# Matmul with bias and tanh on one core: B's first eight k-tiles as whole 128-partition loads, two of them in float32 over SyncE

## The chip, the cores and the metric

The kernel runs on one core of a Trainium2 chip. The metric is the device time of one execution in microseconds (us); several executions are taken and the median is quoted. The profile shows one execution by engine: PE is the matrix engine (PEld are its weight loads), DVE is VectorE, ACT is ScalarE, POOL is GpSimd, SP is SyncE. POOL and SP do no arithmetic that matters here; they issue DMA. "Span" is the profiled execution from first to last instruction.

## The reference

```python
m, k, n = 4096, 4096, 4096
a = np.random.randn(m, k).astype(np.float32)
b = np.random.randn(k, n).astype(np.float32)
bias = np.random.randn(n).astype(np.float32)

def reference(a, b, bias):
    return np.tanh(np.matmul(a, b) + bias)
```

## The kernel before

PE multiplies in float16. A k-tile is 128 values of k, one on each partition, and there are 32 of them. A is cast to float16 by the load, on GpSimd's queue (the input is float32, and a load of 128 x 1024 of its values counts 256 KB in the profile, two bytes a value), lies in memory as rows, and VectorE transposes it in blocks of 32 x 32 (kernels built on this, e1 for one, give right results). So the rows of A are loaded in four quarters of k, `q`, each into 32 partitions, and B has to follow the same order of k: partition `q*32 + p` of k-tile `t` holds `k = q*1024 + t*32 + p`. A k-tile of B therefore takes four DMAs, each into 32 partitions.

The output is made in four chunks of 1024 columns. In the first chunk nothing is on chip yet. There the first eight row-tiles (128 rows each) are taken in two groups of four, so that PE can work on the k-tiles that have arrived: group 0 runs k-tiles 0 to 7 (64 matmuls) and its sums are put aside, group 1 does the same, then group 0 runs k-tiles 8 to 31, then group 1. After that the main loop takes one row-tile at a time.

```python
    def load_b(bt, n0, t0, nt, q):
        src = b[ds(q * KQ + t0 * QP, nt * QP), ds(n0, NCW)]       # KQ = 1024, QP = 32
        nc.gpsimd.dma_start(
            out=bt[t0 // TB][ds(q * QP, QP), ds(t0 % TB, nt), :],
            in_=src.rearrange("(t p) n -> p t n", p=QP),
        )

    def transpose_a(at, an, mb0, t0, nt):
        nc.vector.transpose(
            at[:, ds(t0, nt), :].rearrange("P t (mb p) -> P mb t p", p=QP),
            an[:, ds(mb0, Q), :].rearrange("P mb (t k) -> P mb t k", k=QP),
        )
    ...
    for i in range(WARM):                                         # 24 matmuls of zeros
        nc.tensor.matmul(warm, zeros[:, :P], zeros, start=i == 0, stop=i == WARM - 1)
    want_a("g0a", 2, 0, 2 * Q, 0, KS)                             # A, row-tiles 0 and 1
    want(lambda: load_b_all(0, 2))                                # B, k-tiles 0 and 1
    want_a("g0b", 2, 2 * P, 2 * Q, 0, KS)                         # A, row-tiles 2 and 3
    for t in range(2, KS, 2):
        want(lambda t=t: load_b_all(t, 2))
    bias_bc = biasp.tile([P, NCW], fp32, name="bias_bc")
    want(lambda: load_bias(bias_bc, 0))
    want_a("g1a", 2, 4 * P, 2 * Q, 0, KS)
    ...
    turn(ats[0], "g0a", 0, 0, KS)                                 # turn: transpose
    turn(ats[1], "g0a", Q, 0, KS)
    across(ps, (0, 1), 0, 2, 0)                                   # row-tiles 0, 1; k-tiles 0, 1
    turn(ats[2], "g0b", 0, 0, KS)
    turn(ats[3], "g0b", Q, 0, KS)
    across(ps, (2, 3), 0, 2, 0)
    across(ps, range(G), 2, KS - 4, 0)
    def aside0(ps, m, j):
        put_aside(ps, m, j)                                       # VectorE: sum + bias
        if (m, j) == (1, 1):
            turn1(0)
    down(ps, KS - 2, KS, aside0)
    turn1(1)
    ...
    def end0(ps, m, j):
        end(ps, m, j)
        if (m, j) == (1, 1):
            turn2(0)
    down(ps, KT - TB, KT, end0)
```

`want` puts a load into GpSimd's queue in this order. The loads of A share three buffers.

## Time and profile before

The median was 1791.72 us (1790.18 to 1792.72, three executions).

| what | before |
|---|---|
| span of the profiled execution | 1789.8 us |
| PE busy | 1779.1 us |
| main loop: 7712 matmuls, busy (mean of a start-to-start 215 ns) | 1657.8 us |
| first real matmul | 11.35 us |
| start of the main loop's 7680 matmuls in the chain of waits | 127.84 us |
| from the end of that stretch to the end of the span | 7.76 us |

The last line is the span less 127.84 + 1654.20 us; the last matmuls of the last tile, which is made in two halves, are in it.

PE is busy to 99%, and 8192 matmuls at 215 ns are 1761 us. All that a change can win without touching the matmuls is in the start and the tail. This is PE's timeline of the start (start in us, length, engine, line, operation, count; in brackets PE's idle time before it and what ended it):

```profile
11.35 3.05 PE L121 MATMUL ps<-b,at 128*128 128x512 f16 x8 [2.90 <-DMA b<-in_b_dram]
15.36 14.06 PE L121 MATMUL ps<-b,at 128*128 128x512 f16 x56 [0.95 <-DVE at L83]
30.12 14.05 PE L121 MATMUL ps<-b,atx 128*128 128x512 f16 x64 [0.71 <-DVE atx L83]
44.01 41.60 PE L121 MATMUL ps<-b,at 128*128 128x512 f16 x192
86.23 4.06 PE L121 MATMUL ps<-b,atx 128*128 128x512 f16 x18 [0.62 <-DVE atx L83]
```

The reader is to see four stretches: group 0's first 64 matmuls from 11.35 to 29.4 us, group 1's from 30.12 us, group 0's second part from 44.01 us and group 1's from 86.23 us. The idle time is before the first matmul, between its halves, and before each of group 1's parts. VectorE's groups of instructions, by shape (busy us, mean ns of one, idle before):

```profile
L83 DVE STREAM_TRANSPOSE at<-an 128x1024 f16<-128x1024 f16 x16 | 18.9, 1220 | 26.7 <-DMA an<-in_a_dram 26.7
```

A transpose of eight k-tiles of one row-tile takes 1.22 us. The windows show what each engine does in the first 10 us; the first line names the columns (busy us and count of each engine); the DMA share exceeds 1 in places, and only the GB/s are used here:

```profile
core 0: us, PE busy (x) PEld busy (x) DVE busy (x) ACT busy (x) POOL busy (x), PEclk, DMA share, GB/s
0.00:5.00 5.00, 3.81 (x9) 1.35 (x10) 0.27 (x1) 1.28 (x1) 3.90 (x11) 1.00 0.53 62
5.00:10.00 5.00, 3.45 (x16) 1.40 (x14) 2.17 (x2) 0.00 (x0) 3.63 (x7) 1.00 1.08 143
13.00:14.00 1.00, 1.00 (x4) 0.22 (x2) 0.00 (x0) 0.00 (x0) 0.85 (x2) 0.50 1.22 216
```

The first 10 us move 62 and 143 GB/s. From 30 us on the same view shows 202 to 208 GB/s in every 10 us up to 80 us. At 13 to 14 us PE's granted clock is 0.50, half of full speed. Finally two DMA issues in POOL's timeline:

```profile
60.72 0.54 POOL L66 DMA_DIRECT2D b<-in_b_dram  x1 [0.69 <-DMA b<-in_b_dram]
...
71.07 0.54 POOL L75 DMA_DIRECT2D an<-in_a_dram  x1 [0.69 <-DMA b<-in_b_dram]
```

The first is the last load of B's tiles 24 to 27. The second is eight places later in the queue, and it waited for a load of B. The chain of waits shows the same step elsewhere: the load issued at 42.83 us landed at 52.91 us and released, 0.28 us later, the issue at 53.19 us, which is eight places behind it. So tiles 24 to 27 had landed at about 70.8 us.

### The profile page before, as it was taken

What the parts mean: (1) busy time and instruction counts of PE and PEld (TensorE: products, weight loads), DVE (VectorE), ACT (ScalarE), POOL (GpSimd) and SP (SyncE); (2) the same over time, 40 slices, a digit from 0 to 9 for tenths busy, and PEclk for the clock granted to TensorE, in tenths of its full rate; (3) what the DMA queues carried; (4) which work ended last, traced back from release to release, by engine and by line L of the source; (5) the groups of instructions that cost most, each with busy time, mean ns of one, the idle gap of its engine ahead of it and who ended that gap; (6) DMA issues with size and microseconds to landing.
All of it is one profiled execution on the core that took longest, in us unless ns stands there. A gap on an engine that the chain in (4) does not pass through costs nothing.

```text
span 1789.8 us, 19352 instructions
## 1 busy us (share of the span) xinstructions
PE 1779.1 (99%) x8248; PEld 807.4 (45%) x8248; DVE 745.0 (42%) x420; ACT 162.7 (9%) x260; POOL 358.0 (20%) x668
## 2 busy tenths in 40 slices
PE   8999999999999999999999999999999999999999
PEld 3444444444444444444444444444444444444444
DVE  5463344334433444334433443344334433444341
ACT  0110000000000000000000000000000000000001
POOL 6422222211222211111132222111111111111100
PEclk9999999999999999999999999999999999999999
DMA  9999887665777865655588777555665555655621
GB/s 182 214 189 189 155 159 147 125 132 114 159 147 144 170 140 108 121 119 124 106 168 156 158 142 142 121 112 107 127 120 112 112 113 109 125 112 111 120 70 41
DMA packets 138630, 238.26 MB, mean 133 GB/s; under 512 B 14769, under 2 KB 27569, under 8 KB 138545
## 3 DMA queue, kind: packets, MB, share of 16 engines
q0 software_dynamic: 101248, 169.91, 56.6%
q1 hardware_dynamic: 37296, 67.13, 10.3%
q8 instruction: 64, 1.05, 0.2%
q14 instruction: 22, 0.17, 0.0%
HBM read 337.64 MB, written 67.11 MB: 226 GB/s over the span
## 4 chain that ended last, share of the span: by engine, by line
PE 95%; DMA 4%; POOL 1%; issue 1%; DVE 0%; ACT 0%; ACTq 0%; DVEq 0%; POOLq 0%
PE ps L321 92%; PE ps L121 2%; DMA b<-in_b_dram 2%; DMA an<-in_a_dram 1%; POOL b L66 0%; DMA bias_bc<-in_bias_dram 0%; POOL an L75 0%; DVE atx L83 0%; ACT o_sb L135 0%; DVE o_sb L132 0%; ACTq L354 0%; DVEq L132 0%; POOLq L343 0%
## 5 line engine op out<-in xcount | busy, mean ns | idle before, releaser
L321 PE MATMUL ps<-b,at 128*128 128x512 f16 x7712 | 1657.8, 378 | 0.0
L321 PEld LDWEIGHTS <-at 128*128 128x128 f16 x7712 | 754.6, 98 | 903.3
L132 DVE TENSOR_TENSOR o_sb<-ps,bias_bc 128x512 f32<-128x512 f32 (+1 forms) x243 | 166.4, 686 | 977.8 <-PE ps L321 764.1
L83 DVE STREAM_TRANSPOSE at<-an 128x4096 f16<-128x4096 f16 (+1 forms) x136 | 551.0, 4056 | 26.7 <-DMA an<-in_a_dram 26.7
L75 POOL DMA_DIRECT2D an<-in_a_dram x524 | 282.8, 547 | 1296.6 <-DVE at L83 1224.4
L135 ACT ACTIVATE o_sb<-o_sb 128x512 f32<-128x512 f32 (+1 forms) x243 | 151.5, 624 | 1505.7 <-DVE o_sb L132 1505.7
L66 POOL DMA_DIRECT2D b<-in_b_dram x136 | 73.2, 542 | 55.2 <-PE ps L321 28.6
L121 PE MATMUL ps<-b,at 128*128 128x512 f16 x256 | 58.6, 391 | 3.9 <-DMA b<-in_b_dram 2.9
L121 PE MATMUL ps<-b,atx 128*128 128x512 f16 x256 | 55.7, 379 | 1.3 <-DVE atx L83 1.3
L121 PEld LDWEIGHTS <-at 128*128 128x128 f16 x256 | 25.3, 100 | 37.1 <-issue 5.7
L121 PEld LDWEIGHTS <-atx 128*128 128x128 f16 x256 | 24.8, 98 | 32.2 <-DVE atx L83 2.7
L132 DVE TENSOR_TENSOR spill<-ps,spill 128x512 f32<-128x512 f32 x16 | 10.7, 684 | 25.7 <-PE ps L121 25.4
L135 ACT ACTIVATE spill<-spill 128x512 f32<-128x512 f32 x16 | 10.0, 630 | 117.2 <-DVE spill L132 117.2
L83 DVE STREAM_TRANSPOSE atx<-an 128x1024 f16<-128x1024 f16 (+1 forms) x8 | 18.3, 2295 | 0.0
L155 DVE TENSOR_TENSOR spill<-ps,bias_bc 128x512 f32<-128x512 f32 x16 | 10.1, 670 | 10.0 <-PE ps L121 10.0
L196 PE MATMUL ps<-zeros 128*128 128x512 f16 x24 | 7.3, 476 | 1.2 <-DVE zeros L193 1.2
L196 PEld LDWEIGHTS <-zeros 128*128 128x128 f16 x24 | 2.8, 118 | 5.2 <-issue 2.5
L90 POOL DMA_DIRECT2D bias_bc<-in_bias_dram x4 | 2.3, 563 | 0.1
L135 ACT ACT_TABLE_LOAD x1 | 1.3, 1283 | 0.7 <-PEq L343 0.7
L193 DVE MEMSET zeros<- 128x256 uint32 x1 | 0.3, 272 | 0.9 <-PEq L343 0.9
L343 POOL MEMSET const-float32-0.0<- 128x1 f32 x1 | 0.1, 98 | 0.2 <-issue 0.2
L343 POOL MEMSET const-bfloat16-1.0<- 128x1 bf16 x1 | 0.1, 101 | 0.0
(2 smaller groups left out, 0.2 us busy)
## 6 DMA issues: line engine op xcount, KB each, us to landing
an<-in_a_dram POOLq DMA_DIRECT2D x492, 256.0 KB, 5.4
out_dram<-o_sb SPq DMA_DIRECT2D x239, 256.0 KB, 4.3
b<-in_b_dram POOLq DMA_DIRECT2D x120, 256.0 KB, 8.9
out_dram<-spill SPq DMA_DIRECT2D x16, 256.0 KB, 6.4
an<-in_a_dram POOLq DMA_DIRECT2D x16, 192.0 KB, 7.8
an<-in_a_dram POOLq DMA_DIRECT2D x16, 128.0 KB, 5.7
b<-in_b_dram POOLq DMA_DIRECT2D x16, 128.0 KB, 5.0
bias_bc<-in_bias_dram POOLq DMA_DIRECT2D x4, 512.0 KB, 8.2
```

What stands on the lines that cost most here:

```text
L66: nc.gpsimd.dma_start(out=bt[t0 // TB][ds(q * QP, QP), ds(t0 % TB, nt), :], in_=src.rearrange("(t p) n -> p t n", p=QP),)
L75: nc.gpsimd.dma_start(out=an[ds(q * QP, QP), :, :], in_=src.rearrange("(mb p) k -> p mb k", p=QP),)
L83: nc.vector.transpose(at[:, ds(t0, nt), :].rearrange("P t (mb p) -> P mb t p", p=QP), an[:, ds(mb0, Q), :].rearrange("P mb (t k) -> P mb t ...
L90: nc.gpsimd.dma_start(out=bias_bc, in_=bass.AP(tensor=src.tensor, offset=src.offset, ap=[[0, P], *src.ap]),)
L121: nc.tensor.matmul(ps, at[:, t, :], bt[t // TB][:, t % TB, ts(j, NB)], start=start, stop=stop)
L132: nc.vector.tensor_tensor(out=o_sb[:, piece], in0=ps[:, piece], in1=addend[:, piece], op=mybir.AluOpType.add)
L135: nc.scalar.activation(o_sb[:, piece], o_sb[:, piece], mybir.ActivationFunctionType.Tanh)
L155: nc.vector.tensor_tensor(out=aside(m, j), in0=ps, in1=bias_bc[:, ts(j, NB)], op=mybir.AluOpType.add)
L193: nc.vector.memset(zeros, 0.0)
L196: nc.tensor.matmul(warm, zeros[:, :P], zeros, start=i == 0, stop=i == WARM - 1)
L321: nc.tensor.matmul(ps, at[:, t, :], b_cur[t // TB][:, t % TB, ds(c0, w)], start=t == 0, stop=t == KT - 1,)
L343: nc = _bacc.Bacc("TRN2", target_bir_lowering=False, num_devices=1)
```

## The change

The intent: B's k-tile becomes one DMA into all 128 partitions, if in the first eight k-tiles partition `x` of tile `t` holds `k = x*8 + t`. A quarter of A is then 256 columns of k, and its transpose takes every eighth column. Two of the tiles are loaded in float32 over SyncE, at once, and cast by ScalarE. A's two halves for group 0 come first in GpSimd's queue. ScalarE, not VectorE, puts group 0's sums aside, bias is added later, and the transposes for group 1 move ahead of group 0's last matmuls. The last stores go over two queues. The layout holds for all of A and B, so in the main loop each row-tile of A takes eight loads (256 and 768 columns) and two transposes.

```diff
-    def load_b(bt, n0, t0, nt, q):
-        src = b[ds(q * KQ + t0 * QP, nt * QP), ds(n0, NCW)]
+    def load_b_low(queue, dst, n0, t0, nt):
+        src = b[ds(0, P * KS), ds(n0, NCW)].rearrange("(x t) n -> x t n", t=KS)
+        queue.dma_start(out=dst, in_=src[:, ds(t0, nt), :])
+
+    def load_b(bt, n0, t0, nt, q):
+        src = b[ds(P * KS + (q * (KT - KS) + t0 - KS) * QP, nt * QP), ds(n0, NCW)]
 ...                                          (load_a: the same split; q in the order 0, 2, 1, 3)
-        nc.vector.transpose(
-            at[:, ds(t0, nt), :].rearrange("P t (mb p) -> P mb t p", p=QP),
-            an[:, ds(mb0, Q), :].rearrange("P mb (t k) -> P mb t k", k=QP),
-        )
+        parts = [(0, KS), (KS, t0 + nt - KS)] if t0 < KS < t0 + nt else [(t0, nt)]
+        for t, n in parts:
+            order = "P mb (k t) -> P mb t k" if t < KS else "P mb (t k) -> P mb t k"
+            nc.vector.transpose(
+                at[:, ds(t, n), :].rearrange("P t (mb p) -> P mb t p", p=QP),
+                an[:, ds(mb0, Q), ds((t - t0) * QP, n * QP)].rearrange(order, k=QP),
+            )
 ...
-            nc.sync.dma_start(out=out[ds(mi * P, P), ds(c0 + i * w, w)], in_=o_sb[:, piece])
+            queue.dma_start(out=out[ds(mi * P, P), ds(c0 + i * w, w)], in_=o_sb[:, piece])
 ...
+    def put_aside0(ps, m, j):
+        nc.scalar.copy(aside(m, j), ps)
+    def add_bias(m, j):
+        nc.vector.tensor_tensor(
+            out=aside(m, j), in0=aside(m, j), in1=bias_bc[:, ts(j, NB)], op=mybir.AluOpType.add
+        )
 ...
+    raw_b = spill[3].rearrange("P (h x) n -> P h (x n)", h=RAW)        # RAW = 2
+    for t in range(RAW):
+        load_b_low(nc.sync, raw_b[:, ds(t, 1), :], 0, t, 1)
+        nc.scalar.copy(b_cur[t // TB][:, t % TB, :], raw_b[:, t, :])
 ...
     want_a("g0a", 2, 0, 2 * Q, 0, KS)
-    want(lambda: load_b_all(0, 2))
     want_a("g0b", 2, 2 * P, 2 * Q, 0, KS)
-    for t in range(2, KS, 2):
-        want(lambda t=t: load_b_all(t, 2))
+    for t in range(RAW, KS):
+        want(lambda t=t: load_b_low(nc.gpsimd, b_cur[t // TB][:, ds(t % TB, 1), :], 0, t, 1))
+    want_a("g1a", 2, 4 * P, 2 * Q, 0, KS)
     bias_bc = biasp.tile([P, NCW], fp32, name="bias_bc")
-    want(lambda: load_bias(bias_bc, 0))
-    want_a("g1a", 2, 4 * P, 2 * Q, 0, KS)
+    want(lambda: load_bias(bias_bc, 0, nc.gpsimd))
 ...
-    def aside0(ps, m, j):
-        put_aside(ps, m, j)
-        if (m, j) == (1, 1):
-            turn1(0)
-    down(ps, KS - 2, KS, aside0)
-    turn1(1)
+    turn1(0)
+    turn1(1)
+    down(ps, KS - 2, KS, put_aside0)
 ...
-    down(ps, KT - TB, KT, end0)
+    turn2(0)
+    down(ps, KT - TB, KT, end)
 ...
+                queues = (nc.sync, nc.scalar) if halves > 1 else (nc.sync,)
```

More of the change, by code (lines that the diff above doesn't have):

```diff
@@ L34 @@
     assert (M, K, K2, N) == (4096, 4096, 4096, 4096)
-    KQ = K // Q
     KT = K // P
@@ L44 @@
     KS = 8
+    RAW = 2
     AN = 3
@@ L72, in load_a, with load_bias @@
         an = anat.tile([P, nmb, nt * QP], fp16, name="an")
-        for q in range(Q):
-            src = a[ds(m0, nmb * QP), ds(q * KQ + t0 * QP, nt * QP)]
-            nc.gpsimd.dma_start(
-                out=an[ds(q * QP, QP), :, :],
-                in_=src.rearrange("(mb p) k -> p mb k", p=QP),
-            )
+        parts = [(0, KS), (KS, t0 + nt - KS)] if t0 < KS < t0 + nt else [(t0, nt)]
+        for t, n in parts:
+            for q in (0, 2, 1, 3):
+                k = q * KS * QP if t < KS else P * KS + (q * (KT - KS) + t - KS) * QP
+                src = a[ds(m0, nmb * QP), ds(k, n * QP)]
+                nc.gpsimd.dma_start(
+                    out=an[ds(q * QP, QP), :, ds((t - t0) * QP, n * QP)],
+                    in_=src.rearrange("(mb p) k -> p mb k", p=QP),
+                )
         return an
     def transpose_a(at, an, mb0, t0, nt):
-        nc.vector.transpose(
-            at[:, ds(t0, nt), :].rearrange("P t (mb p) -> P mb t p", p=QP),
-            an[:, ds(mb0, Q), :].rearrange("P mb (t k) -> P mb t k", k=QP),
-        )
-    def load_bias(bias_bc, n0):
+        parts = [(0, KS), (KS, t0 + nt - KS)] if t0 < KS < t0 + nt else [(t0, nt)]
+        for t, n in parts:
+            order = "P mb (k t) -> P mb t k" if t < KS else "P mb (t k) -> P mb t k"
[3 more added lines that the diff above has]
+            )
+    def load_bias(bias_bc, n0, queue):
         src = bias[ds(n0, NCW)]
-        nc.gpsimd.dma_start(
+        queue.dma_start(
             out=bias_bc,
@@ L123, in mm, with finish @@
         )
-    def finish(ps, addend, mi, c0, w=NB, o_sb=None, pieces=1):
+    def finish(ps, addend, mi, c0, w=NB, o_sb=None, queues=(nc.sync,)):
         if o_sb is None:
             o_sb = opool.tile([P, w], fp32, name="o_sb")
-        w //= pieces
-        for i in range(pieces):
+        w //= len(queues)
+        for i, queue in enumerate(queues):
             piece = ds(i * w, w)
@@ L152, in aside, with put_aside1 @@
         return spill[(m * J + j) // 4][:, (m * J + j) % 4, :]
-    def put_aside(ps, m, j):
+    def put_aside0(ps, m, j):
[3 more added lines that the diff above has]
+            out=aside(m, j), in0=aside(m, j), in1=bias_bc[:, ts(j, NB)], op=mybir.AluOpType.add
+        )
+    def put_aside1(ps, m, j):
         nc.vector.tensor_tensor(
@@ L165, in load_b_all @@
     def load_b_all(t0, nt):
-        for q in range(Q):
+        for q in (0, 2, 1, 3):
             load_b(b_cur, 0, t0, nt, q)
@@ L217 @@
     ps = banks()
-    turn(ats[0], "g0a", 0, 0, KS)
-    turn(ats[1], "g0a", Q, 0, KS)
-    across(ps, (0, 1), 0, 2, 0)
-    turn(ats[2], "g0b", 0, 0, KS)
-    turn(ats[3], "g0b", Q, 0, KS)
-    across(ps, (2, 3), 0, 2, 0)
-    across(ps, range(G), 2, KS - 4, 0)
+    for m in range(2):
+        turn(ats[m], "g0a", m * Q, 0, KS)
+    across(ps, (0, 1), 0, RAW, 0)
+    for m in range(2):
+        turn(ats[2 + m], "g0b", m * Q, 0, KS)
+    across(ps, (2, 3), 0, RAW, 0)
+    across(ps, range(G), RAW, KS - 2 - RAW, 0)
     def turn1(m):
         turn(ats[G + m], "g1a" if m < 2 else "g1b", (m % 2) * Q, 0, KS)
-    def aside0(ps, m, j):
-        put_aside(ps, m, j)
-        if (m, j) == (1, 1):
-            turn1(0)
-    down(ps, KS - 2, KS, aside0)
+    turn1(0)
     turn1(1)
+    down(ps, KS - 2, KS, put_aside0)
     def turn0(t, m):
@@ L247, in before1 @@
             turn0(KS, 2 + j)
-    group1(0, KS, put_aside, before1)
+    group1(0, KS, put_aside1, before1)
     ps = banks()
     for t in range(KS, KT, TA):
-        if t > KS:
-            for m in range(G):
+        for m in range(G):
+            if t > KS:
                 turn0(t, m)
+            else:
+                for j in range(J):
+                    add_bias(m, j)
         across(ps, range(G), t, TA - TB if t + TA == KT else TA, KS)
@@ L260, in turn2 @@
         turn(ats[G + m], ("g1", m), 0, KS, KT - KS)
-    def end0(ps, m, j):
-        end(ps, m, j)
-        if (m, j) == (1, 1):
-            turn2(0)
-    down(ps, KT - TB, KT, end0)
+    turn2(0)
+    down(ps, KT - TB, KT, end)
     ahead = 3
@@ L299 @@
             b_next = new_b()
-            left = [(s, q) for s in range(KT // TB) for q in range(Q)]
+            left = [(s, None) for s in range(KS // TB)]
+            left += [(s, q) for s in range(KS // TB, KT // TB) for q in range(Q)]
         if i + ahead < len(todo):
@@ L303 @@
         for s, q in left[:2]:
-            want(lambda s=s, q=q, c=c, bt=b_next: load_b(bt, (c + 1) * NCW, s * TB, TB, q))
+            if q is None:
+                want(lambda s=s, c=c, bt=b_next: load_b_low(
+                    nc.gpsimd, bt[s], (c + 1) * NCW, s * TB, TB))
+            else:
+                want(lambda s=s, q=q, c=c, bt=b_next: load_b(
+                    bt, (c + 1) * NCW, s * TB, TB, q))
         left = left[2:]
@@ L307 @@
             bias_next = biasp.tile([P, NCW], fp32, name="bias_bc")
-            want(lambda c=c, bb=bias_next: load_bias(bb, (c + 1) * NCW))
+            want(lambda c=c, bb=bias_next: load_bias(bb, (c + 1) * NCW, nc.gpsimd))
         pump()
@@ L327 @@
                     )
-                finish(ps, bias_bc[:, ds(c0, w)], mi, c * NCW + c0, w, pieces=halves)
+                queues = (nc.sync, nc.scalar) if halves > 1 else (nc.sync,)
+                finish(ps, bias_bc[:, ds(c0, w)], mi, c * NCW + c0, w, queues=queues)
 _INS = ['a', 'b', 'bias']
```

## The prediction

> **What bounds it now.** TensorE: the chain of waits is 92% the main loop's matmuls, and the windows show no idle PE from 86.2 to 1782 us. 7712 matmuls in 1657.8 us are 215 ns each; 8192 make 1761 us of the 1789.8 us span. At most 28 us lie in start and tail, so 2% (36 us) is out of reach. In the start the timeline shows:
> - first real matmul at 11.35 us (it waits for B), after 2.9 us of idle PE; then half clock (0.50) until 18.6 us, at 427 ns a matmul, and about 2 us of waits for the transposes of row-tiles 2 and 3.
> - group 0's first 64 matmuls end at 29.41 us (64 x 215 ns would be 13.8 us). Gaps of 0.7 and 0.4 us follow, and one of 0.6 us at 85.6 us, where the last transpose stands behind four additions on VectorE.
> - yet DMA is saturated all that time: 256 KB every 1.27 to 1.33 us (206 GB/s). B's tiles 24 to 27 are issued last at 60.7 us; the issue eight places later, at 71.07 us, shows them landed about 70.7 us; PE needs them at about 71.8 us. The slack is only about 1 us.
>
> **What the change does.** Matmuls stay the same. Two B tiles (1 MB float32) go over SyncE, before 1.3 us; two ScalarE casts are added (about 1.1 us each, an estimate from 0.63 us for 512 columns). A's second half precedes B's rest, and six 256 KB loads replace twelve of 128 KB. First matmul at about 9.5 us (A landed at 7.8 us, now shared with raw B; transpose 1.2 us). PE's idle falls to 1 to 2 us, so the clock probably stays full; [...] here 2.9 us was enough. Group 0's first part should end at 24 to 26 us, 4 to 5 us earlier. ScalarE's copies and earlier transposes remove the 0.7 and 0.6 us gaps.
>
> **How much counts.** Most of those 5 us run into the DMA stream: PE can come only 1 us nearer to B's tiles 24 to 27. The bytes read stay the same, [...] so the second queue wins only the ramp: the first 10 us moved 62 and 143 GB/s against 206, about 1 MB or 5 us short, part of it latency. I expect 2 us of it back (1 to 4). Gain: 2 + 1 us in the start, 0.6 us for the last gap, 0.2 us in the tail (second queue for the last store): about 3.8 us.
>
> In the main loop each A row costs eight issues, not four (POOL +270 us, an estimate from 547 ns), smaller packets, and two transposes (1.2 + 3.4 us against 4.4). DMA is at 55 to 85% there, three rows ahead: hidden, no gain or loss.
>
> **Prediction:** 1787.9 us, 8 in 10 within 1785.0 to 1790.8. Faster by over 2%: 0.01; within 2%: 0.98; slower: 0.01.
>
> **Signs.** Right: first matmul at 9 to 10 us, no half clock after it; group 0's first part ends near 25 us; PE then stalls 1 to 2 us on B between 35 and 70 us; group 1's second part starts near 82.5 us (86.2 before). Wrong if: raw B delays A so that PE falls to half clock; the transposes that read with stride 8 run slower than 1.2 us; the DMA stream itself gets faster (128-partition loads), which gives 5 to 7 us; or small A packets starve rows after 100 us.

(The 2.9 us in the text is the idle PE before the first real matmul, 2.90 us, after which the kernel before went to half clock; the latency it mentions was 5.0 us in the median from issue to landing for the loads of 128 KB of B.) 2 + 1 + 0.6 + 0.2 us came to about 3.8 us, which takes the 1791.72 us of the kernel before to 1787.9 us.

## The result

The median is 1788.41 us (1787.97 to 1789.1, four executions) against 1792.14 us of the kernel before in the same rounds. The ratio is 0.9981 with a 95% interval of 0.9964 to 0.9999. A ratio here is the mean time of one kernel's runs over that of the other's of the same rounds, so it is not quite the ratio of the medians quoted. The gain of about 3.4 us (0.19% of 1792 us) lies inside the predicted range.

PE's timeline of the start, after:

```profile
11.19 0.60 PE L134 MATMUL ps<-b,at 128*128 128x512 f16 x2 [1.90 <-DVE at L96]
13.05 3.10 PE L134 MATMUL ps<-b,at 128*128 128x512 f16 x8 [1.26 <-DVE at L96]
16.80 11.91 PE L134 MATMUL ps<-b,at 128*128 128x512 f16 x54 [0.66 <-DVE at L96]
28.55 13.98 PE L134 MATMUL ps<-b,atx 128*128 128x512 f16 x64
42.37 41.60 PE L134 MATMUL ps<-b,at 128*128 128x512 f16 x192
83.81 6.42 PE L134 MATMUL ps<-b,atx 128*128 128x512 f16 x29
```

Three things are to be seen. The first real matmul starts at 11.19 us, almost as before, not at 9.5 us. Up to 16.8 us PE does 10 of its 64 matmuls (16 + 48 would have been the plan) and waits for VectorE three times. From 16.80 us on there is no idle time at all: no wait for B, and no gaps before 28.55 and 83.81 us. The chain of waits says the same in two lines (start, length, what):

```profile
16.80 108.61 PE ps L134 x502
125.41 1654.20 PE ps L349 x7680
```

The main loop starts at 125.41 us against 127.84 us. These 2.43 us are the gain of the start, and the four starts of PE's stretches in the two timelines divide it: 0.86 us in group 0's first part (its end, before the gap, 29.41 us before; 28.55 us after), 0.71 us for the gap before group 1, 0.07 us in group 1's first part (44.01 less 30.12 against 42.37 less 28.55), 0.78 us in group 0's second part with the gap behind it (42.22 against 41.44 us). The span fell by 3.1 us; the remaining 0.67 us are after the main loop's 7680 matmuls (7.09 against 7.76 us).

One part of this is not the change's own. The windows (of half a microsecond) show a granted clock of 0.50 for 6.83 us in the profiled execution before (12.0 to 18.8 us), and for 3.42 us after (13.6 to 17.0 us). Before, it lay on the 56 matmuls from 15.36 us: they took 14.06 us, about 1.8 us more than at the pace of e6 below, which had no half clock (54 in 11.83 us). After, the 54 from 16.80 us took 11.91 us, 0.1 us more. So at full clock, and with no other wait in its place, group 0's first part would have ended about 0.9 us later after the change than before (an estimate from these numbers): the 0.86 us come from the clock of this pair of executions, and the loads and transposes together gained nothing here. The other 1.6 us lie at the two gaps. How the gain of the medians divides is not shown; other executions have other clocks (means of 0.998 to 1.000 before, 0.998 or 0.999 after).

VectorE, by shape:

```profile
L96 DVE STREAM_TRANSPOSE at<-an 128x1024 f16<-128x1024 f16 x136 | 264.1, 1947 | 17.9 <-DMA an<-in_a_dram 17.9
```

and in its timeline:

```profile
9.16 7.58 DVE L96 STREAM_TRANSPOSE at<-an 128x1024 f16<-128x1024 f16 x4 [8.03 <-DMA an<-in_a_dram]
```

The transposes with 1024 columns now take 1.95 us in the mean, and in that group of 136 the 12 of k-tiles 8 to 31 still read contiguous columns. Group 0's four first ones stand in a row from 9.16 us for 7.58 us, which is 1.90 us each. The windows of the first 10 us:

```profile
0.00:5.00 5.00, 3.81 (x9) 1.34 (x10) 0.27 (x1) 1.63 (x2) 3.90 (x11) 1.00 0.65 209
5.00:10.00 5.00, 4.29 (x16) 1.62 (x14) 0.84 (x1) 1.74 (x2) 3.18 (x6) 1.00 1.39 184
```

and ScalarE's two casts of raw B in its timeline:

```profile
4.65 1.05 ACT L217 CAST b<-spill 128x1024 f16<-128x1024 f32 x1 [2.63 <-DMA spill<-in_b_dram]
5.85 1.05 ACT L217 CAST b<-spill 128x1024 f16<-128x1024 f32 x1 [0.16 <-DMA spill<-in_b_dram]
```

The bytes moved went from 62 to 209 GB/s in the first 5 us (raw B counts four bytes a value here, 512 KB for a k-tile of 128 x 1024 values, a cast load two, 256 KB). B's first two tiles were ready at 6.9 us, more than 4 us before PE could use them: A's first half landed at 9.16 us, 1.3 us later than before (7.83 us), and was the last to come. Last, the two DMA issues:

```profile
57.30 0.55 POOL L72 DMA_DIRECT2D b<-in_b_dram  x1 [0.68 <-DMA b<-in_b_dram]
...
67.67 0.55 POOL L85 DMA_DIRECT2D an<-in_a_dram  x1 [0.68 <-DMA b<-in_b_dram]
```

B's tiles 24 to 27 were issued last at 57.30 us, 3.4 us earlier than before, and had landed by about 67.4 us. PE needs them at about 69.95 us (42.37 us plus 128 x 0.2155 us). The slack has grown from about 1 us to about 2.5 us.

### The profile page after: what moved, and what is told of

Same layout as the page of the kernel before. It is cut to its first block, busy times and chain, and to the rows that moved or that the text cites. A ratio compares the mean times of both kernels' runs of the same rounds, so it can differ in the third digit from the quotient of the medians.

```text
span 1786.7 us, 20163 instructions
## 1 busy us (share of the span) xinstructions
PE 1778.1 (100%) x8248; PEld 807.6 (45%) x8248; DVE 852.4 (48%) x540; ACT 169.2 (9%) x270; POOL 603.8 (34%) x1120
## 2 busy tenths in 40 slices
DMA packets 207340, 238.87 MB, mean 134 GB/s; under 512 B 22032, under 2 KB 157712, under 8 KB 207248
## 4 chain that ended last, share of the span: by engine, by line
PE 99%; DMA 0%; issue 0%; DVE 0%; POOL 0%; ACT 0%; DVEq 0%; POOLq 0%
PE ps L349 93%; PE ps L134 6%; DMA an<-in_a_dram 0%; POOL an L85 0%; DVE at L96 0%; ACT o_sb L148 0%; DVE o_sb L145 0%; DVEq L96 0%; DVEq L145 0%; POOLq L372 0%
## 5 line engine op out<-in xcount | busy, mean ns | idle before, releaser
L85 POOL DMA_DIRECT2D an<-in_a_dram x1004 | 542.0, 547 | 1064.8 <-DVE at L96 932.1
L96 DVE STREAM_TRANSPOSE at<-an 128x1024 f16<-128x1024 f16 (+1 forms) x256 | 655.2, 2600 | 17.9 <-DMA an<-in_a_dram 17.9
L72 POOL DMA_DIRECT2D b<-in_b_dram x96 | 52.1, 545 | 18.9 <-DMA an<-in_a_dram 10.5
L68 POOL DMA_DIRECT2D b<-in_b_dram x12 | 7.7, 646 | 24.5 <-PE ps L349 22.3
L176 DVE TENSOR_TENSOR spill<-ps,bias_bc 128x512 f32<-128x512 f32 x8 | 5.4, 671 | 3.4 <-DMA an<-in_a_dram 2.1
L168 ACT COPY spill<-ps 128x512 f32<-128x512 f32 x8 | 4.0, 623 | 18.8 <-PE ps L134 18.8
L171 DVE TENSOR_TENSOR spill<-spill,bias_bc 128x512 f32<-128x512 f32 x8 | 4.9, 684 | 0.0
```

Source lines behind the costliest of these rows:

```text
L68: queue.dma_start(out=dst, in_=src[:, ds(t0, nt), :])
L72: nc.gpsimd.dma_start(out=bt[t0 // TB][ds(q * QP, QP), ds(t0 % TB, nt), :], in_=src.rearrange("(t p) n -> p t n", p=QP),)
L85: nc.gpsimd.dma_start(out=an[ds(q * QP, QP), :, ds((t - t0) * QP, n * QP)], in_=src.rearrange("(mb p) k -> p mb k", p=QP),)
L96: nc.vector.transpose(at[:, ds(t, n), :].rearrange("P t (mb p) -> P mb t p", p=QP), an[:, ds(mb0, Q), ds((t - t0) * QP, n * QP)].rearrange ...
L168: nc.scalar.copy(aside(m, j), ps)
L171: nc.vector.tensor_tensor(out=aside(m, j), in0=aside(m, j), in1=bias_bc[:, ts(j, NB)], op=mybir.AluOpType.add)
```

## The experiments

Each was run with the kernel before beside it, five executions for its median; e1 to e4, e5 to e8, and e9 to e12 each shared a chip and the runs of the kernel before. "Loop" is the start of the main loop's 7680 matmuls in its own profiled execution, "issue" the last issue of B's tiles 24 to 27, "wait" PE's wait for a load of B after 60 us. All were right except the one that is wrong on purpose.

| kernel | median (range), us | before beside it, us | ratio (95% interval) | loop, us | issue, us | wait, us |
|---|---|---|---|---|---|---|
| before | 1791.72 | | | 127.84 | 60.72 | none |
| after | 1788.41 (1787.97 to 1789.1) | 1792.14 | 0.9981 (0.9964 to 0.9999) | 125.41 | 57.30 | none |
| e1_order_only | 1790.33 (1788.77 to 1791.06) | 1791.43 | 0.9992 (0.998 to 1.0005) | 126.56 | 61.02 | see text |
| e2_no_stride | 1786.45 (1785.84 to 1786.77) | 1791.43 | 0.9972 (0.9958 to 0.9986) | 122.75 | 57.12 | 0.21 |
| e3_old_tail | 1788.55 (1788.52 to 1790.34) | 1791.43 | 0.9985 (0.9973 to 0.9998) | 126.99 | 57.19 | none |
| e4_one_queue | 1791.49 (1790.95 to 1791.71) | 1791.43 | 0.9999 (0.9987 to 1.0012) | 128.44 | 59.99 | none |
| e5_old_layout | 1788.56 (1788.16 to 1788.8) | 1791.56 | 0.9985 (0.9973 to 0.9998) | 125.29 | 59.68 | 0.68 |
| e6_longer_warm | 1788.20 (1787.84 to 1788.56) | 1791.56 | 0.9983 (0.997 to 0.9996) | 125.03 | 57.25 | none |
| e7_split | 1788.64 (1788.06 to 1789.96) | 1791.56 | 0.9987 (0.9974 to 0.9999) | 124.65 | 59.02 | 1.96 |
| e8_bias_late | 1788.11 (1787.51 to 1789.48) | 1791.56 | 0.9985 (0.9971 to 0.9998) | 124.09 | 57.74 | 0.33 |
| e9_raw_quadrants | 1789.87 (1789.39 to 1790.87) | 1791.71 | 0.999 (0.9977 to 1.0002) | 126.91 | 58.26 | none |
| e10_raw_columns | 1790.85 (1790.39 to 1791.78) | 1791.71 | 0.9995 (0.9983 to 1.0008) | 128.44 | 59.38 | none |
| e12_low_quadrants | 1788.99 (1788.33 to 1790.3) | 1791.71 | 0.9983 (0.9969 to 0.9996) | 127.20 | 57.81 | none |
| e11_start | 1785.93 (1785.43 to 1786.17) | 1791.71 | 0.9966 (0.9954 to 0.9979) | 122.63 | 56.91 | 0.82 |

The differences are fractions of a per cent and the executions of one kernel spread over 0.6 to 2.5 us. The time less the span is 1.7 to 1.8 us in all kernels but e5, e7 and e8, where it is 2.2 us; the trace does not show where those 0.4 us are, and it stays open.

The half clock has to be watched as well. In the profiled executions the windows show 3.42 us of it for the changed kernel and 6.83 us for the kernel before, and the windows of 5 us give about 3.4 us in e5 and e8, 6.8 to 6.9 us in e9 and e12, 10.2 us in e10 and none in e7 and e11: close to one, two or three times 3.42 us. The mean clock of the whole execution is 0.999 in those with one such length, 0.998 with two and 0.997 with three; it is 0.998 in e1, e3 and e4, and 1.0 in e2 and e6. In e4 the half clock came in two pieces: PE did 6 matmuls in 2.74 us from 12.66 us, two in 0.60 us from 16.37 us and 54 in 13.52 us from 18.23 us, where e6 did 6 in 1.47, two in 0.60 and 54 in 11.83 us. So where PE has work and no other wait, a piece costs about 1.7 us (13.52 less 11.83 us in e4), half its length. Half clock came after 2.90 us of idle PE (before), after waits of 1.90 and 1.26 us (after) and after 2.30 us (e5), and not after 2.09 us (e7). e3 and e12 begin like the changed kernel and have one piece more, so it also differs from execution to execution.

### e1: only the order

```diff
 (the kernel before)
+    turn1(0); turn1(1)
-    down(ps, KS - 2, KS, aside0); turn1(1)
+    down(ps, KS - 2, KS, put_aside0)          # ScalarE's copy; VectorE adds bias at k-tile 8
-    down(ps, KT - TB, KT, end0)
+    turn2(0)
+    down(ps, KT - TB, KT, end)
```

> The kernel before with only the order changed: both transposes for group 1 ahead of the last two k-tiles of group 0, ScalarE puts group 0's sums aside, the bias is added later, the last big transpose ahead of group 0's additions. Old layout, no SyncE loads, old tail. Theory 1 (the change's gain of 2.4 us in the start is mostly these gaps): the gaps of 0.71, 0.38 and 0.62 us in PE go, the main loop starts 1.5 to 1.8 us earlier than before, the time falls by about 1.7 us. Theory 2 (the DMA stream limits the start, as I predicted): PE can come at most about 1 us nearer to B's tiles 24 to 27; PE waits on B appear between 44 and 80 us and the gain is at most 1.0 us.

The main loop started 1.28 us earlier (126.56 against 127.84 us; half clock alike in both, as the 56 matmuls at 15.4 us took 14.15 and 14.06 us) and the median fell by 1.1 us. Both idle gaps are gone from PE's timeline. Neither theory is met to the letter: less than theory 1's 1.5 to 1.8 us, more than theory 2's 1.0 us. The chain of waits explains it, which ran through B's tiles 24 to 27 and on to PE:

```profile
61.02 10.08 DMA b<-in_b_dram
...
71.14 55.41 PE ps L121 x256
```

The last of these tiles was issued at 61.02 us and released PE at 71.14 us. (The stretch in which that falls took 41.65 us, from 43.30 to 84.95 us, against 41.44 us in the changed kernel: some 0.2 us lost.) Without any help to the DMA stream, the new order alone brings PE right up to it. About half of the change's 2.43 us in the start can be had this way; this run does not show that the same share came from it in the changed kernel.

### e2: the stride taken away

```diff
 (the changed kernel; the result is wrong on purpose)
-            order = "P mb (k t) -> P mb t k" if t < KS else "P mb (t k) -> P mb t k"
+            order = "P mb (t k) -> P mb t k"
```

> The changed kernel with one thing taken back on purpose against correctness: the low eight k-tiles of A are transposed from contiguous 32-column blocks (wrong result, k-tiles of A and B no longer match). Theory 1: the low transposes fall from 1.9 to 1.2 us each, four of them stand in a row before group 0's third row-tile can start, so group 0's first 64 matmuls end 2 to 2.5 us earlier (near 26.2 us instead of 28.4), and as B's tiles 24 to 27 land 2.4 us before PE needs them in the changed kernel, nearly all of it stays: main loop starts 2 to 2.4 us earlier, time 1.8 to 2.4 us lower than the changed kernel (about 5.5 us under the kernel before). Theory 2 (DMA stream limits): the start of group 0 comes earlier, but PE then waits on B, and the time falls by less than 1 us. The main loop's length doesn't change in either.

Every instruction is where it was in the changed kernel; only the columns that a transpose reads differ. VectorE's group of these transposes, and then PE's timeline:

```profile
L96 DVE STREAM_TRANSPOSE at<-an 128x1024 f16<-128x1024 f16 x136 | 167.0, 1233 | 20.6 <-DMA an<-in_a_dram 20.6
```

```profile
10.00 0.60 PE L134 MATMUL ps<-b,at 128*128 128x512 f16 x2 [1.10 <-DVE at L96]
...
25.52 13.98 PE L134 MATMUL ps<-b,atx 128*128 128x512 f16 x64
39.33 27.79 PE L134 MATMUL ps<-b,at 128*128 128x512 f16 x128
67.34 13.97 PE L134 MATMUL ps<-b,at 128*128 128x512 f16 x64 [0.21 <-DMA b<-in_b_dram]
```

The same 136 transposes take 1.23 us in the mean, so the stride alone made them 1.95. The first matmul starts at 10.00 us, group 1 at 25.52 instead of 28.55 us, group 0's second part at 39.33 instead of 42.37 us. (The half clock, absent here with a mean clock of 1.0, has little part in this: the last 54 matmuls already start at 13.85 instead of 16.80 us.) These 3.0 us are more than the slack of about 2.5 us that the changed kernel left, and at 67.34 us PE waits 0.21 us for B, the first such wait. The main loop starts 2.66 us earlier than in the changed kernel. The median is 2.1 us under that of e3, which shared its rounds and differs from the changed kernel only in the tail. Theory 1 holds, and the stride costs about 2 us of the time.

For one transpose of 128 x 1024 float16 values that is 1.23 us from contiguous columns and 1.90 to 2.01 us at a stride of eight values (1.90 us for group 0's four; 2.01 us is (264.1 less 12 x 1.235) us over 124). Why the stride costs this is not shown, and other strides were not tested.

### e3: the old tail

```diff
 (the changed kernel)
-                queues = (nc.sync, nc.scalar) if halves > 1 else (nc.sync,)
+                queues = (nc.sync, nc.sync) if halves > 1 else (nc.sync,)
```

> The changed kernel with both halves of the last stores on SyncE as before. The time from the last matmul of the first half to the end was 7.76 us before and 7.09 us after, so the measured expectation is plus 0.6 to 0.7 us against the changed kernel, all of it after the last matmul; my prediction had 0.2 us.

This missed. The tail after the main loop's 7680 matmuls was 7.31 us here, 0.22 us more than in the changed kernel, and the median 0.14 us more. The kernels with one queue at the end had 7.76, 7.84 (e1) and 7.31 us, the eleven with two 6.95 to 7.26 us. So the second queue is worth something between 0.1 and 0.7 us, and these runs don't settle it.

The profiled execution of e3 took 1790.34 us, the other four 1788.5 to 1788.7 us. Its PE needed 13.79 us for the 54 matmuls from 16.51 us on, which the changed kernel did in 11.91 us: half clock lasted longer in it (mean clock 0.998; 0.999 in the other four). That is the spread of these executions.

### e4: everything on one queue

```diff
 (the changed kernel)
-    for t in range(RAW):
-        load_b_low(nc.sync, raw_b[:, ds(t, 1), :], 0, t, 1)
-        nc.scalar.copy(b_cur[t // TB][:, t % TB, :], raw_b[:, t, :])
     want_a("g0a", 2, 0, 2 * Q, 0, KS)
+    (B's k-tiles 0 and 1, cast, on GpSimd's queue)
     want_a("g0b", 2, 2 * P, 2 * Q, 0, KS)
```

> The changed kernel without SyncE's float32 loads: B's k-tiles 0 and 1 are cast by GpSimd's queue, between A's first and second half, as before; the layout with stride 8 stays. Theory 1 (VectorE's strided transposes set the start): A's first half lands 1.3 us earlier (7.8 us, no raw B beside it), the first matmul starts near 9.8 instead of 11.2 us, A's second half lands near 13 us, group 0's first part ends within 1 us of the changed kernel's 28.4 us; B's tiles 24 to 27 come 2 to 3 us later, which uses up the slack of 2.4 us; the time is within 1 us of the changed kernel. Theory 2 (the second queue wins ramp time of the DMA stream, and that is the gain): PE waits on B after 30 us and the time is 2 to 3 us higher.

Theory 2's time, but not by theory 2's wait. The whole gain was gone (ratio 0.9999), and PE never waited for B. What happened is in VectorE's timeline:

```profile
8.78 3.83 DVE L96 STREAM_TRANSPOSE at<-an 128x1024 f16<-128x1024 f16 x2 [7.64 <-DMA an<-in_a_dram]
14.33 3.84 DVE L96 STREAM_TRANSPOSE at<-an 128x1024 f16<-128x1024 f16 x2 [1.73 <-DMA an<-in_a_dram]
```

A's first half came hardly earlier than in the changed kernel (8.78 against 9.16 us; kernels with the same raw loads, e2, e3, e6, e11 and e12, had 8.70 to 9.23 us), so it is not raw B that delays it against the kernel before. But its second half landed at 14.33 us, behind B's two tiles. In the changed kernel the chain of waits has it landed at 11.76 us, before VectorE was done with the first half (12.97 us, two transposes after 9.16 us). From 14.33 us two more strided transposes last to 18.2 us, where the changed kernel was done at 16.74 us. DMA issues of the stream were late as well (59.99 against 57.30 us for the last of tiles 24 to 27). So SyncE's two loads do two things: they take 0.5 MB of cast loads (2.5 us at 206 GB/s) out of the way of A's second half, and they move their own 1 MB in the first 10 us, when the queue alone moved only 63 and 145 GB/s in this run.

That is not the whole loss. From the last wait for VectorE to the main loop the chain of waits has the same 502 matmuls as in the changed kernel:

```profile
18.23 110.21 PE ps L134 x502
```

They start 1.43 us later (18.23 against 16.80 us) and take 1.60 us longer (110.21 against 108.61 us) without a wait. The half clock does this; its second piece lies on the first 54 of them, which took 13.52 us against 11.91 us. It was no accident of the profile: e4's five executions all have a mean clock of 0.997 or 0.998, three of the changed kernel's four 0.999. So of the 3.0 us about half is VectorE's later work and half the longer half clock.

From 30 to 80 us the stream runs at 202 to 208 GB/s in the kernel before and at 202 to 210 GB/s in the changed kernel, and the loads are mostly issued 1.2 to 1.4 us apart (25 of 36 and 24 of 35 gaps); no second queue loads there, so what one could add to it is not shown. For the first 10 us the second queue was worth 2.7 us of the stream and 3.0 us of the main loop's start: 1.4 us because A's second half no longer stood behind B, and 1.6 us of half clock. Issue time explains only a part: issuing the two tiles before A's second half took GpSimd 1.12 us, and A's second half landed 2.5 us later (14.25 against 11.76 us).

### e5: all of the change except the layout

```diff
 (the kernel before, with the order of e1, the new tail, bias behind g1a, and)
+    for q in range(Q):
+        nc.sync.dma_start(
+            out=raw_b[ds(q * QP, QP), :, :],
+            in_=b[ds(q * KQ, 2 * QP), ds(0, NCW)].rearrange("(t p) n -> p t n", p=QP),
+        )
+    for t in range(2):
+        nc.scalar.copy(b_cur[0][:, t, :], raw_b[:, t, :])
```

> All of the change except its layout: k-tiles as in the kernel before (contiguous transposes, 32-partition loads of B), with the two float32 tiles over SyncE, A first, ScalarE's copies, the new order and tail; a right result. Theory 1 (the layout's only effect that counts is the stride, which costs about 2 us in the start): like the wrong-result run without stride: first matmul near 10 us, group 0's first part ends near 25.5 us, PE waits at most 0.5 us on B near 67 us, time 1786 to 1787 us. Theory 2 (one 128-partition load per k-tile is what makes B come sooner): B's tiles 2 to 7 land 1 to 2 us later than in the changed kernel, PE waits on B before 25 us, and the time is 1788 us or more.

Theory 1 fell here. With contiguous transposes and a right result I expected 1786 to 1787 us; it took 1788.56 us, as much as the changed kernel (ratios 0.9985 and 0.9981). The transposes were fast, but everything before them was later: raw B at 8.57 instead of 5.85 us, A's first half at 10.10 us, and the last of B's tiles 24 to 27 was issued at 59.68 us, 2.6 us later than in e2. PE waited 0.68 us for them. In the first 5 us DMA moved 141 GB/s instead of 209. So the layout has a gain, in the loads, and a cost, in the transposes, and they cancel within these runs: from e2 to e5 the loads' gain is lost (2.1 us by the medians, 2.5 us by the start of the main loop), from e2 to the changed kernel the stride's cost is added (2.0 and 2.7 us).

### e6: a longer warm-up

```diff
 (the changed kernel)
-    WARM = 24
+    WARM = 33
```

> The changed kernel with 33 instead of 24 matmuls of zeros, which fill PE's idle 1.9 us before its first real matmul; nothing else changes. Theory 1 (transposes on VectorE set the start, the half clock only adds a part that differs from run to run: 54 matmuls after 16.8 us took 11.91 us in one run and 13.79 us in another of the same start): no half clock after 11 us, the median falls by 0.2 to 0.7 us and the highest run by 1 to 2 us. Theory 2 (the half clock is the main loss in the start): 1.5 us or more off the median. A third, that the dummies delay the first matmul: plus 0 to 0.5 us.

PE's idle before the first real matmul vanished, and the 54 matmuls from 16.5 us took 11.83 us, which is full clock. The median is 1788.20 us, the range 0.7 us. Theory 1: in the changed kernel the half clock is worth little in most executions, since PE waits for the transposes anyhow, and up to 1.96 us in the worst (13.79 us in e3 less 11.83 us here).

### e7 and e8: an earlier first matmul, and bias later

```diff
 (e7 = e5, with)
+    for g, m0 in (("g0a", 0), ("g0b", 2)):
+        for m in range(2):
+            turn(ats[m0 + m], g, m * Q, 0, 2)
+        for m in range(2):
+            turn(ats[m0 + m], g, m * Q, 2, KS - 2, 2)
 (e8 = e7, with)
             want(lambda u=u: load_b_all(u, TB))
+            if u == KT - 2 * TB:
+                want(lambda: load_bias(bias_bc, 0))     # and VectorE adds bias from then on
```

> e5_old_layout with each transpose of group 0's first part cut in two, k-tiles 0 and 1 of both row-tiles ahead of 2 to 7. First matmul near 9.2 us and group 0's first part ends near 23.5 us, 2 us earlier than e5. Theory 1 (with the stride gone the DMA stream is the limit, B's tiles 24 to 27): PE then waits on B for about 2 us near 67 us and the time stays within 0.4 us of e5. Theory 2 (the start is worth what it gains): 2 us off e5, about 1784.5 us.

> e7_split with the 512 KB broadcast of bias moved behind B's tiles 24 to 27 (ScalarE puts both groups' sums aside without bias, VectorE adds it later). Theory 1 (the DMA stream is the limit): all B tiles up to 27 land 1.7 to 2 us sooner, the wait near 67 us is gone or moves to B's tiles 28 to 31 and is under 1 us, the time falls 1.2 to 2 us against e7, to about 1784.8 us, the fastest of all. Theory 2 (DMA isn't the limit in e7): same time as e7.

In e7 the first matmul came at 10.89 us, not at 9.2 us, because ScalarE's casts of the late raw B were not done (they ran from 9.79 to 11.78 us, behind a load of the activation table at 8.50 us). Group 1 still started 2 us earlier than in e5 (25.62 against 27.60 us); about 1.7 us of this (an estimate: half its length) is e5's half clock of about 3.4 us, from a mean clock of 0.82 and 0.84 in the windows at 10 and 15 us, which e7 did not have (1.00 in both). Then PE lost most of it:

```profile
25.62 13.98 PE L124 MATMUL ps<-b,atx 128*128 128x512 f16 x64
...
69.24 13.97 PE L124 MATMUL ps<-b,at 128*128 128x512 f16 x64 [1.96 <-DMA b<-in_b_dram]
```

A wait of 1.96 us for B at 69.24 us, and a time equal to e5's. This is the DMA limit of the prediction, met where the start no longer hides it. In e8 bias (512 KB) comes behind B's tiles 24 to 27: they were issued 1.28 us earlier, the wait fell to 0.33 us, the main loop started 0.56 us earlier, and the median fell by 0.5 us, less than the 1.2 to 2 us expected. PE's timeline of e8 shows why:

```profile
68.26 13.97 PE L124 MATMUL ps<-b,at 128*128 128x512 f16 x64 [0.33 <-DMA b<-in_b_dram]
82.49 7.71 PE L124 MATMUL ps<-b,atx 128*128 128x512 f16 x35 [0.26 <-DVE spill L135]
```

Theory 1 is right in kind. PE had B's tiles 24 to 27 0.98 us sooner than in e7 (68.26 against 69.24 us), but lost 0.42 us of it before group 1's second part, where it now waits for VectorE: a transpose of A stands there ahead of the additions that free PE's sums, and could only start when its load had landed, at 78.49 us. The chain of waits has that load issued at 70.36 us, when bias had landed. So bias now stands in front of A instead of B. (Group 1's first part started 0.7 us later than in e7, at 26.33 us, because e8's execution had about 3.4 us of half clock, from a mean clock of 0.66 from 10 to 15 us; that only shortened the wait for B.)

### e9 and e10: the same 1 MB of raw B in four loads

```diff
 (e9: the changed kernel, with)
-    for t in range(RAW):
-        load_b_low(nc.sync, raw_b[:, ds(t, 1), :], 0, t, 1)
+    for q in range(Q):
+        nc.sync.dma_start(out=raw_b[ds(q * QP, QP), :, :], in_=low[ds(q * QP, QP), ds(0, RAW), :])
 (e10: the changed kernel, with)
+    for t in range(RAW):
+        for h in range(2):
+            nc.sync.dma_start(out=raw_b[:, ds(t, 1), ts(h, NB)], in_=low[:, ds(t, 1), ts(h, NB)])
```

> The changed kernel with the same 1 MB of float32 B over SyncE, as four loads of 32 partitions (two k-tiles each, 256 KB) in place of two of 128 partitions. Theory A (loads into 32 partitions move slower than into 128): raw B lands near 8.5 us instead of 5.8, A's first half near 10 instead of 9.0 us, first 5 us move about 140 GB/s instead of 209, B's tiles from 8 on are issued 1 to 1.5 us later than 24.4 us, PE starts about 1 us later: plus 0.7 to 1.3 us. Theory B (number and pace of loads only): like the changed kernel within 0.4 us, raw B landed by 6.5 us.

> Control for e9: also four loads of 256 KB over SyncE, but each into all 128 partitions (half a k-tile's columns, 2 KB rows). Theory A: like the changed kernel, raw B landed by 6.5 us, time within 0.4 us. Theory B (four issues are slower than two): like e9.

e9 came out as theory A said: raw B landed at 8.33 us, A's first half at 9.98 us, the first 5 us moved 142 GB/s, and the main loop started 1.5 us later than in the changed kernel. But its control speaks against theory A as the reason. e10's loads go into all 128 partitions, and it is still slower than e9. These lines of the timelines show the end of the wait for raw B on ScalarE (in e9 a load of the activation table comes first) and for A's first half on VectorE, first of e9, then of e10:

```profile
8.33 1.28 ACT L219 ACT_TABLE_LOAD   x1 [8.33 <-DMA spill<-in_b_dram]
```

```profile
9.98 7.63 DVE L96 STREAM_TRANSPOSE at<-an 128x1024 f16<-128x1024 f16 x4 [8.84 <-DMA an<-in_a_dram]
```

```profile
9.26 1.04 ACT L220 CAST b<-spill 128x1024 f16<-128x1024 f32 x1 [2.79 <-DMA spill<-in_b_dram]
```

```profile
11.17 7.59 DVE L96 STREAM_TRANSPOSE at<-an 128x1024 f16<-128x1024 f16 x4 [10.03 <-DMA an<-in_a_dram]
```

In e10 the second raw tile was there only at 9.26 us and A's first half at 11.17 us, 2.0 us later than in the changed kernel. (Not all of the time is these landings: the last 502 matmuls start 0.86 us later in e9 and 2.02 us later in e10 than in the changed kernel, and take 0.64 and 1.02 us longer, by half clock: their first 54 took 12.55 and 12.93 us against 11.91 us.) So 32 partitions against 128 is not what makes the loads in e5 and e9 late, or not alone. What e5, e9 and e10 share is four loads of 256 KB on SyncE, issued from 0.75 to 2.55 us, instead of two of 512 KB issued from 0.75 to 1.61 us. Whether it is the number of loads, their size or the later issue, and how they hold up GpSimd's loads of A, stays open. (e10 also has rows of 2 KB instead of 4 KB, which may be why it is the slower one; that was not tested.) What is settled is that two whole k-tiles, as the change loads them, are the best of the four forms tried.

### e12: GpSimd's loads of B's tiles 2 to 7 in quarters

```diff
 (the changed kernel: six loads of 128 partitions become twelve of 32, two k-tiles each)
+        for q in (0, 2, 1, 3):
+            nc.gpsimd.dma_start(
+                out=b_cur[t // TB][ds(q * QP, QP), ds(t % TB, 2), :],
+                in_=low[ds(q * QP, QP), ds(t, 2), :],
+            )
```

> The changed kernel with GpSimd's six 256 KB loads of B's tiles 2 to 7 into 128 partitions replaced by twelve of 128 KB into 32 partitions, same layout. Theory A (32-partition loads and their 0.67 us issues slow the stream): B's tiles from 8 on are issued 0.7 to 1.5 us later than 24.4 us; B's tiles 24 to 27 had 2.4 us to spare, so the time rises by less than 0.5 us. If B's tiles 2 to 7 themselves come too late for PE before 28 us, plus 0.5 to 1.5 us. Theory B (the loads' form doesn't matter): issue times and time unchanged.

B's tile 8 was first issued at 25.48 instead of 24.45 us, tiles 24 to 27 last at 57.81 instead of 57.30 us; the ratio is 0.9983 against 0.9981. Theory A with its first branch: half to one us of the stream, which PE's slack hides. (Its profiled execution had the long half clock: 13.65 us for 54 matmuls, which is why its main loop starts 1.8 us later; the mean clock was 0.998 in four of its five executions.) If the delays of the last issue of tiles 24 to 27 add up, those of e9 (0.96 us) and e12 (0.51 us) make 1.5 of the 2.4 us by which e5 is behind the changed kernel; the rest is not explained.

### e11: a version that beats both

```diff
 (the changed kernel, with)
+    for m, t0, nt in ((0, 0, RAW), (1, 0, RAW), (0, RAW, KS - RAW), (2, 0, RAW), (3, 0, RAW),
+                      (1, RAW, KS - RAW), (2, RAW, KS - RAW), (3, RAW, KS - RAW)):
+        turn(ats[m], "g0a" if m < 2 else "g0b", (m % 2) * Q, t0, nt)     # transposes cut in two
+    across(ps, (0, 1), 0, RAW, 0)
+    across(ps, (2, 3), 0, RAW, 0)
+    across(ps, (0, 1), RAW, KS - 2 - RAW, 0)
+    across(ps, (2, 3), RAW, KS - 2 - RAW, 0)
 (and bias behind B's tiles 24 to 27, as in e8)
```

> A version meant to beat both: the changed kernel with group 0's first transposes cut in two (k-tiles 0 and 1 first, about 0.5 us each), row-tiles 0 and 1 taken through k-tiles 2 to 5 ahead of 2 and 3, and bias loaded after B's tiles 24 to 27. First matmul near 9.7 us, group 0's first part ends near 24.5 to 25.5 us (28.4 in the changed kernel), B's tiles 24 to 27 come about 2 us sooner than there, so that PE waits less than 0.5 us on B: main loop starts 3 to 4 us earlier, time 1784 to 1785.5 us. If the DMA stream limits more than I think: no better than 1786.4 us, the run without the stride.

```profile
9.46 1.99 PE L143 MATMUL ps<-b,at 128*128 128x512 f16 x8 [0.34 <-DVE at L92]
12.18 12.34 PE L143 MATMUL ps<-b,at 128*128 128x512 f16 x56 [0.73 <-DVE at L92]
24.36 13.98 PE L143 MATMUL ps<-b,atx 128*128 128x512 f16 x64
...
66.78 13.97 PE L143 MATMUL ps<-b,at 128*128 128x512 f16 x64 [0.82 <-DMA b<-in_b_dram]
```

The first matmul starts at 9.46 us, group 1 at 24.36 us, 4.2 us earlier than in the changed kernel. At 66.78 us PE waits 0.82 us for B. The median is 1785.93 us, 2.5 us under the changed kernel's and 5.8 us under that of the kernel before in the same rounds (ratio 0.9966, interval 0.9954 to 0.9979). That is a little above the range expected: the wait for B was 0.82 and not under 0.5 us, and PE lost another 0.44 us before group 1's second part (81.03 us), waiting for VectorE behind A and bias as in e8. The profiled execution had no half clock (mean clock 1.0). How much each of its edits brings was not separated.

## Why the prediction was right, point by point

- **The time, 1787.9 us (1785.0 to 1790.8): right**, 1788.41 us measured. So was the claim that 2% is out of reach: PE is busy for 1778.1 of 1786.7 us.
- **First matmul "at about 9.5 us": wrong**, 11.19 us. Two terms were mis-sized. "A landed at 7.8 us, now shared with raw B" was 9.16 us. Its reason is not shown either: e4 has no raw B and A's first half at 8.78 us; what delays A by about 1 us against the kernel before (the order of its quarters, their new place side by side in A's rows, or the larger loads behind it) stays open. And "transpose 1.2 us" was 1.90 us, which the prediction had named among the things that would make it wrong. e2 shows that the stride is the cause and that it costs about 2 us.
- **"The clock probably stays full": wrong.** The changed kernel's windows show a mean clock of 0.86 from 10 to 15 us and 0.80 from 15 to 20 us: 3.42 us at 0.50, where the kernel before had 6.83 us. PE was idle for 1.90 and 1.26 us before it, 3.2 us where 1 to 2 us were forecast. e6 shows that this costs the changed kernel's median little.
- **"Group 0's first part should end at 24 to 26 us": wrong**, 28.55 us, for the same two terms. Without the stride it ended at 25.5 us (e2).
- **The DMA stream as the limit, "PE then stalls 1 to 2 us on B between 35 and 70 us": this step failed for the changed kernel.** PE never waited for B. The stream came forward by 3.4 us (57.30 against 60.72 us), not by "2 us", and PE by only 1.6 us (42.37 against 44.01 us), so that the slack grew. The limit itself is real: it released PE in e1, took 0.21 us in e2, 0.68 in e5 and 1.96 in e7, as soon as the start was faster or the stream slower. In the changed kernel the limit of the start is VectorE, behind A.
- **"The second queue wins only the ramp ... 2 us of it back (1 to 4)": right.** e4 puts it at 2.7 us of the stream.
- **The gain as "2 + 1 us in the start, 0.6 us for the last gap, 0.2 us in the tail": the sum is right, its terms are not.** Start and gaps together measured 2.43 us (3.6 predicted), the tail 0.67 us in the profiled pair, of which e3 confirms only 0.1 to 0.2 us. The two errors in the start worked against each other: too little time for A and its transposes, and a limit by B that was not reached. That the total came out close is to this extent luck, and so is the profiled pair's 0.86 us in group 0's first part, which the clock gave.
- **The main loop "hidden, no gain or loss": right.** Its 7680 matmuls take 1654.20 us in both chains of waits. GpSimd's busy time rose by 246 us (603.8 against 358.0; 270 predicted), DMA's share from 0.74 to 0.83 between 130 and 700 us, with PE busy throughout. The packets did get smaller: 157712 of 207340 were under 2 KB, against 27569 of 138630.

## What to carry to other kernels

A new layout has two ends: price the transposes that read it as well as the loads that write it. Here whole-tile loads won about 2 us and a stride of eight float16 values in the transposes lost about 2 us (1.23 against 1.90 to 2.01 us each). When a start is a race of several chains (A and its transposes, B, the queue), find the slack of each before adding up gains, and test it by making the shortest faster; the next one shows up at once, as B did in e2 and e7 (waits of 0.21 and 1.96 us). When two traces differ by a microsecond or two, compare their half clock before explaining the rest. And a control with one thing changed is worth its run: e9 alone would have told a false story about partitions.
